# Series of products with a moving operand taken by turns, put behind the last product of a two-layer model

## The chip, the cores and the metric

The kernel runs on one core of one Trainium2 chip. The metric is the device time of one execution in microseconds. All of the work is in float32, and nearly all products use the fp32r form of it, in which one instruction streams a moving operand of up to 512 columns through a stationary operand of 128 × 128.

## The reference

The model has two layers over 256 tokens of width 1024, with a memory of another 256 tokens. Every layer has four parts, each followed by a layer normalisation:

```python
for l in range(DEPTH):
    h = layer_norm(ALPHA * h + 0.5 * swiglu(h, ffn1_gate[l], ffn1_up[l], ffn1_down[l]), ln_g[l, 0], ln_b[l, 0])
    z = h @ w_in[l]
    cb, cc, ch, rq, rf, ri, rg, pu = jnp.split(z, split_at, axis=-1)
    y_conv = short_gated_conv(ch, cb, cc, conv_w[l])
    y_rec = hgrn2(rq, rf, ri, rg, lbs[l], rec_norm_g[l])
    y_pool = multiscale_pool(pu, pool_w[l], pool_scale[l])
    mix = jnp.concatenate([y_conv, y_rec, y_pool], axis=-1) @ w_out[l]
    h = layer_norm(ALPHA * h + mix, ln_g[l, 1], ln_b[l, 1])
    h = layer_norm(ALPHA * h + cross_attn(h, mem, ca_q[l], ca_k[l], ca_v[l], ca_o[l]), ln_g[l, 2], ln_b[l, 2])
    h = layer_norm(ALPHA * h + 0.5 * swiglu(h, ffn2_gate[l], ffn2_up[l], ffn2_down[l]), ln_g[l, 3], ln_b[l, 3])
return h
```

`swiglu` is `(silu(x @ w_gate) * (x @ w_up)) @ w_down` with an inner width of 2816. `hgrn2` is a gated recurrence over the tokens, `multiscale_pool` takes running means over 2, 4, 8 and 16 tokens, and `cross_attn` attends to the memory with four heads.

## The kernel before

Every float32 operand is kept as two fp32r tiles, a high part and what is left of it, the low part (`split`, lines 59 and 60: ScalarE rounds the high part, VectorE subtracts it). A product of two such operands is made of three: high by high, high by low and low by high.

The activations `h` (two tiles of 128 tokens) are transposed by TensorE into `xT`, a tile of 128 partitions by 8 slices of 128 features, each with the high part of 256 tokens and then the low part of 256 tokens. `mT` holds the memory in the same way. So one slice of `xT` or `mT` is a run of 512 elements in a partition: elements 0 to 255 are the high part and 256 to 511 the low part.

```python
xT = cst.tile([P, NK, 2, SEQ], F32R, name="xT")
mT = cst.tile([P, NK, 2, SEQ], F32R, name="mT")
```

The weights come from memory by the queue of SP, in pieces of 1 MB, into three rotating tiles `raw`, and are split into `whi` and `wlo`. Two helpers make most products. `mm_cols` (lines 97 to 100) has the weights stationary and one slice of `xT` moving: eight products of 512 columns by the high weights (both parts of the activations at once) and eight of 256 columns by the low weights, into one PSUM tile, whose two halves are added afterwards. `mm_rows` (lines 109 to 111) has the activations stationary and 512 columns of the weights moving. In both, the moving operand is one unbroken run of elements in each partition, and so is the output in PSUM. Every product loads its stationary operand anew.

Inside the recurrence (line 578) TensorE also multiplies plain fp32 operands of 128 columns; there the moving operand is a view of `q` in runs of 1, 2, 4 and up to 64 elements, one length for each of seven levels, with gaps of the same length between the runs.

PSUM has four buffers with the tag `acc` and four with the tag `dn`, each of 512 float32 columns, which take turns. A planner orders the instructions of each engine by their dependencies; where `tc.manual_schedule` names an engine, its instructions stay in the order in which they are written.

The last thing that the kernel computes is `finish` (from line 247) of the second feed-forward part of layer 1. It makes the last products of the down projection for the first 128 tokens, normalises these and writes them out, and does the same for the other 128 tokens, where the last 512 columns are made in two pieces of 256 (lines 231 to 235). After the last of these products TensorE has no more work, while VectorE finishes the second normalisation and the output is written by the queues of SP and ScalarE (line 294).

Of the kernel before, what the change touches and what calls it, by code (L numbers as in the profile page):

```python
# [14 lines left out]
E = mybir.EngineType  # L15
PSUM = bass.MemoryType.PSUM

P = 128
# [783 lines left out]
        pend = ffn(l, "ffn2", 3, pend, last=l == DEPTH - 1)  # L802


# [1 line left out]
_INS = [  # L806
    "x", "mem", "ffn1_gate", "ffn1_up", "ffn1_down", "w_in", "conv_w", "rec_lb", "rec_norm_g", "pool_w",
# [22 lines left out]
```

## Time and profile before

| | |
|---|---|
| time, median of 2 runs | 1176.38 us (1175.93 to 1176.84) |
| time of the profiled execution | 1176.58 us |
| span of the profiled execution | 1174.8 us |
| mean granted clock of TensorE | 0.998 |
| TensorE products | 6219, busy 1161.9 us |
| TensorE weight loads | 6219, busy 1001.2 us |
| VectorE busy | 824.7 us |
| ScalarE busy | 595.6 us |
| moved by DMA | 218.23 MB |

Lines of a group have the line of the kernel, the engine, the operation, the output and the inputs by the program's names, the shapes and the number of instructions; behind these stand the busy time and the mean of one. Lines in order of time have the start in us from the span's start, the duration in us, the engine and then the same names. "acc<-xT,whi" is a product into a tile `acc` with `xT` moving and `whi` stationary. Records of products overlap, since one product starts before the last column of the one before it has reached PSUM: the time that a product costs in a stream is the distance between two starts.

### The profile page before, as it was taken

What the parts mean: (1) busy time and instruction counts of PE and PEld (TensorE: products, weight loads), DVE (VectorE), ACT (ScalarE), POOL (GpSimd) and SP (SyncE); (2) the same over time, 40 slices, a digit from 0 to 9 for tenths busy, and PEclk for the clock granted to TensorE, in tenths of its full rate; (3) what the DMA queues carried; (4) which work ended last, traced back from release to release, by engine and by line L of the source; (5) the groups of instructions that cost most, each with busy time, mean ns of one, the idle gap of its engine ahead of it and who ended that gap; (6) DMA issues with size and microseconds to landing.
All of it is one profiled execution on the core that took longest, in us unless ns stands there. A gap on an engine that the chain in (4) does not pass through costs nothing.

```text
span 1174.8 us, 15745 instructions
## 1 busy us (share of the span) xinstructions
PE 1161.9 (99%) x6219; PEld 1001.2 (85%) x6219; DVE 824.7 (70%) x1194; ACT 595.6 (51%) x873; POOL 40.1 (3%) x80
## 2 busy tenths in 40 slices
PE   8999999999999999999999999999999999999997
PEld 6888888888889888888888888888888888888886
DVE  5766567889787666566677665687998777665665
ACT  6555553626456355455355555446354653554550
POOL 7000000000000000000000000000000000000000
PEclk9999999999999999999999999999999999999999
DMA  8655564644474375655466544655255545655440
GB/s 327 252 193 201 174 221 143 220 140 151 172 244 167 96 247 180 215 198 196 144 215 221 202 168 169 228 187 194 73 209 183 212 144 177 217 179 203 164 171 36
DMA packets 98522, 218.23 MB, mean 186 GB/s; under 512 B 3792, under 2 KB 16368, under 8 KB 98448
## 3 DMA queue, kind: packets, MB, share of 16 engines
q1 hardware_dynamic: 97968, 216.68, 53.2%
q8 instruction: 49, 0.80, 0.3%
q10 hardware_dynamic: 288, 0.39, 0.1%
q14 instruction: 25, 0.20, 0.0%
q0 software_dynamic: 192, 0.15, 0.0%
HBM read 216.15 MB, written 1.05 MB: 185 GB/s over the span
## 4 chain that ended last, share of the span: by engine, by line
PE 97%; DVE 2%; DMA 0%; ACT 0%; issue 0%; SPq 0%; DVEq 0%; ACTq 0%
PE acc L97 29%; PE acc L99 17%; PE dn L111 10%; PE dn L109 10%; PE dn L110 9%; PE acc L109 5%; PE acc L110 5%; PE acc L111 5%; PE acc L100 4%; PE acc L149 1%; PE dn L578 1%; DMA raw<-in_ffn_gate_dram 0%; DVE wlo L60 0%; DVE AT L597 0%; PE dn L621 0%; PE acc L759 0%
## 5 line engine op out<-in xcount | busy, mean ns | idle before, releaser
L60 DVE TENSOR_TENSOR wlo<-raw,whi 128x1024 fp32r<-128x1024 f32 (+1 forms) x396 | 471.1, 1209 | 129.7 <-ACT whi L59 73.6
L59 ACT CAST whi<-raw 128x1024 fp32r<-128x1024 f32 (+1 forms) x396 | 399.7, 1043 | 208.2 <-PE dn L111 140.9
L97 PE MATMUL acc<-xT,whi 128*128 128x512 f32 x1400 | 358.5, 393 | 0.0
L97 PEld LDWEIGHTS acc<-xT,whi 128*128 128x128 f32 x1400 | 262.2, 188 | 50.3
L99 PEld LDWEIGHTS acc<-xT,wlo 128*128 128x128 f32 x1600 | 218.3, 190 | 15.5
L99 PE MATMUL acc<-xT,wlo 128*128 128x256 f32 x1600 | 223.5, 282 | 0.0
L109 PE MATMUL dn<-whi,ah 128*128 128x512 f32 x346 | 135.3, 391 | 0.0
L111 PE MATMUL dn<-whi,al 128*128 128x512 f32 x346 | 134.8, 389 | 0.0
L110 PE MATMUL dn<-wlo,ah 128*128 128x512 f32 x346 | 134.6, 389 | 0.0
L105 DVE TENSOR_TENSOR sg<-acc,sg 128x256 f32<-128x256 f32 x72 | 30.4, 422 | 78.4 <-ACT sg L104 78.4
L100 PE MATMUL acc<-xT,whi 128*128 128x512 f32 x200 | 79.2, 396 | 0.0
L111 PEld LDWEIGHTS dn<-whi,al 128*128 128x128 f32 x346 | 64.9, 188 | 13.7
L110 PEld LDWEIGHTS dn<-wlo,ah 128*128 128x128 f32 x346 | 65.0, 188 | 13.5
L109 PEld LDWEIGHTS dn<-whi,ah 128*128 128x128 f32 x346 | 65.1, 188 | 12.6
L104 ACT COPY sg<-acc 128x256 f32<-128x256 f32 x72 | 26.6, 370 | 94.7 <-PE acc L100 94.7
L109 PE MATMUL acc<-whi,xT 128*128 128x512 f32 x160 | 63.4, 397 | 0.1
L110 PE MATMUL acc<-wlo,xT 128*128 128x512 f32 x160 | 63.0, 393 | 0.0
L111 PE MATMUL acc<-whi,xT 128*128 128x512 f32 x160 | 62.8, 392 | 0.0
L104 ACT COPY up<-acc 128x256 f32<-128x256 f32 x72 | 26.6, 370 | 59.8 <-PE acc L100 59.8
L105 DVE TENSOR_TENSOR up<-acc,up 128x256 f32<-128x256 f32 x72 | 30.3, 421 | 31.8 <-ACT up L104 31.8
L109 PE MATMUL dn<-whi,xT 128*128 128x512 f32 x128 | 50.3, 393 | 0.0
L111 PE MATMUL dn<-whi,xT 128*128 128x512 f32 x128 | 49.9, 390 | 0.0
(202 smaller groups left out, 1236.9 us busy)
## 6 DMA issues: line engine op xcount, KB each, us to landing
raw<-in_ffn_up_dram SPq DMA_DIRECT2D x44, 1024.0 KB, 5.0
raw<-in_ffn_down_dram SPq DMA_DIRECT2D x44, 1024.0 KB, 4.8
raw<-in_ffn_gate_dram SPq DMA_DIRECT2D x42, 1024.0 KB, 5.0
raw<-in_w_in_dram SPq DMA_DIRECT2D x24, 1024.0 KB, 5.0
raw<-in_ca_k_dram SPq DMA_DIRECT2D x8, 1024.0 KB, 4.9
raw<-in_w_out_dram SPq DMA_DIRECT2D x8, 1024.0 KB, 4.8
raw<-in_ca_v_dram SPq DMA_DIRECT2D x8, 1024.0 KB, 5.6
raw<-in_ca_q_dram SPq DMA_DIRECT2D x8, 1024.0 KB, 4.9
```

The source lines that it names most:

```text
L59: nc.scalar.copy(hi, src)
L60: nc.vector.tensor_tensor(lo, src, hi.bitcast(F32), op=ALU.subtract)
L97: nc.tensor.matmul(o, w.at(k, cols)[0], x[:, k], start=k == 0, stop=False)
L99: nc.tensor.matmul(o[:, 0, :], w.at(k, cols)[1], x[:, k, 0, :], start=False, stop=False)
L100: nc.tensor.matmul(o, w.at(NK - 1, cols)[0], x[:, NK - 1], start=False, stop=True)
L104: nc.scalar.copy(dst, view(o[:, 1, :]))
L105: nc.vector.tensor_tensor(dst, view(o[:, 0, :]), dst, op=ALU.add)
L109: nc.tensor.matmul(o, xh, wh, start=start, stop=False)
L110: nc.tensor.matmul(o, xh, wl, start=False, stop=False)
L111: nc.tensor.matmul(o, xl, wh, start=False, stop=stop)
L149: nc.tensor.transpose(pt[:, k, :], src[:, (4 * j + k) * P : (4 * j + k + 1) * P], unit)
L578: nc.tensor.matmul(o[:, hh], kc[:, hh, :], view(qf, hh * P + c, (other - c, 2), (2 * c, a), (1, c)), start=True, stop=True,)
```

## The change

Behind the two layers, a block is added in which TensorE runs products that write one PSUM tile `o` of 512 columns; nothing reads that tile. The stationary operand is always 128 columns of `xT` and the moving operand a view of `mT`, both as the run of the kernel has left them. A view is a list of (step, count) pairs, the outermost first. `series` makes 12 products of one kind, over six slices of `mT` and seven of `xT`; there are 24 calls. `turns`, which is `[(1, 256), (256, 2)]`, takes one element of the high part, one of the low part, the next of the high part, and so on: 512 columns in ones from two stretches. `both` does this in runs of `c` elements, for `c` = 2, 4, 8 and 16; the second call for each `c` gives the output the same order, so that every column lands where it would have without the turns. Four further series take ones from stretches that are 16, 32, 64 and 128 elements apart. One takes pairs from two slices, 512 apart. Five have 256 columns, two of them in pairs (of which one is in effect an unbroken run) and three in ones. Three series have a stationary operand with a step of two elements: with `turns`, with an unbroken run, and with 256 columns in ones. The last series has 128 columns in one run.

After the series come 48 products: `h` stands for eight of 512 columns in `turns`, `n` for eight of 256 columns in ones with other stationary columns; first they alternate, and then they run in the order h, n, h, n by eights.

```diff
+    x1, m1 = (a.rearrange("p k h s -> p (k h s)") for a in (xT, mT))
+
+    def view(t, at, dims):
+        return bass.AP(tensor=t.tensor, offset=t.offset + at, ap=[list(t.ap[0])] + [list(d) for d in dims])
+
+    def series(dims, odims=None, n=12, w=((1, P),), slow=False):
+        ncol = 1
+        for d in dims:
+            ncol *= d[1]
+        for k in range(n):
+            b = 512 * (k % 6)
+            out = view(o, 0, odims or [(1, ncol)])
+            nc.tensor.matmul(out, view(x1, 512 * (k % 7), w), view(m1, b, dims), start=True, stop=True)
+
+    with tc.manual_schedule(engines={E.PE}):
+        o = acc((P, 512))
+        turns = [(1, 256), (256, 2)]
+        series([(1, 512)])
+        series(turns)
+        for c in (2, 4, 8, 16):
+            both = [(c, 256 // c), (256, 2), (1, c)]
+            series(both)
+            series(both, both)
+        series([(32, 16), (1, 16), (16, 2)])
+        series([(64, 8), (1, 32), (32, 2)])
+        series([(128, 4), (1, 64), (64, 2)])
+        series([(256, 2), (1, 128), (128, 2)])
+        series([(2, 128), (512, 2), (1, 2)])
+        series([(1, 128), (256, 2)])
+        series([(1, 128), (128, 2)])
+        series([(2, 128), (1, 2)])
+        series([(2, 64), (128, 2), (1, 2)])
+        series([(32, 8), (1, 16), (16, 2)])
+        series(turns, w=((2, 128),))
+        series([(1, 512)], w=((2, 128),))
+        series([(1, 128), (128, 2)], w=((2, 128),))
+        series([(1, 128)])
+        h = [(view(o, 0, [(1, 512)]), view(x1, 512 * (k % 7), [(1, P)]), view(m1, 512 * k, turns)) for k in range(8)]
+        n = [
+            (view(o, 0, [(1, 256)]), view(x1, 512 * (k % 7) + 256, [(1, P)]), view(m1, 512 * k, [(1, 128), (256, 2)]))
+            for k in range(8)
+        ]
+        for m in [m for k in range(8) for m in (h[k], n[k])] + h + n + h + n:
+            nc.tensor.matmul(*m, start=True, stop=True)
```

## The prediction

> **What bounds the kernel now.** I read the page from the top: the busy shares, the clock row of the 40 slices, and the chain that ended last.
>
> ```profile
> span 1174.8 us, 15745 instructions
> PE 1161.9 (99%) x6219; PEld 1001.2 (85%) x6219; DVE 824.7 (70%) x1194; ACT 595.6 (51%) x873; POOL 40.1 (3%) x80
> PEclk9999999999999999999999999999999999999999
> ...
> PE 97%; DVE 2%; DMA 0%; ACT 0%; issue 0%; SPq 0%; DVEq 0%; ACTq 0%
> ```
>
> TensorE is busy for 99% of the span and makes 97% of the chain. Whatever is put on its queue lengthens the kernel, unless it fits where TensorE is idle. So I asked for the waits of TensorE, and for the order of time around its last product.
>
> ```profile
> PE acc L149 <- DMA h<-in_x_dram: 4.8, 3, 3.4
> PE dn L578 <- DVE kc L572: 0.6, 2, 0.3
> ```
>
> Its waits are 5.4 us in all, most of them at the start. The only other idle stretch is behind the last product:
>
> ```profile
> 1163.01 0.28 PE L109 MATMUL acc<-whi,ah 128*128 128x256 f32 x1
> ...
> 1167.21 0.28 PE L111 MATMUL acc<-whi,al 128*128 128x256 f32 x1
> 1167.52 0.42 DVE L269 TENSOR_TENSOR h<-h,acc 128x256 f32<-128x256 f32 x1 [1.27 <-PE acc L111]
> 1167.98 0.43 DVE L279 BATCH_NORM_STATS2 st<-h 128x6 f32<-128x256 f32 x1
> ...
> 1170.13 1.54 DVE L291 SCALAR_TENSOR_TENSOR h<-h,rs,lnb 128x512 f32<-128x512 f32 x3
> 1170.90 1.13 SPq L294 DMA_DIRECT2D out_dram<-h  x2
> ```
>
> The last product starts at 1167.21 and its record ends at 1167.49; the last normalisation and the write of the output follow until 1174.8. These 7.3 us are the cover of the added work: the new products read nothing that the tail writes, and the tail reads nothing of theirs.
>
> **What is added.** Nothing is removed or moved. Each of the 24 series has 12 products. By the number of moving columns (the product of the counts in the pattern): 17 series have 512 columns, 6 have 256 and one has 128. The mixed run at the end has three rounds of the eight `h` (512 columns) and the eight `n` (256 columns). That makes 17 × 12 + 24 = **228 products of 512 columns**, 6 × 12 + 24 = **96 of 256** and **12 of 128**, together 336, each with its own weight load.
>
> The price of one is the distance from start to start, not the duration of a record, since records overlap. For 512 columns, from a stretch where the products follow each other without a wait:
>
> ```profile
> 1123.26 0.40 PE L109 MATMUL dn<-whi,ah 128*128 128x512 f32 x1
> ...
> 1133.93 0.39 PE L111 MATMUL dn<-whi,al 128*128 128x512 f32 x1
> ```
>
> These are the first and the last of 48 such rows: 10.67 us in 47 steps, 0.227 us each. For 256 columns the rows at 1163.01 and 1167.21 above are the first and the last of 36: 4.20 us in 35 steps, 0.120 us each. The difference is 0.107 us for 256 columns, or 0.418 ns a column, on top of some 0.013 us that each product costs. For 128 columns of this type there is no row. The nearest is the decay product, of plain fp32, which leaves two records for each product:
>
> ```profile
> 836.18 1.05 PE L578 MATMUL dn<-q,kc 128*128 128x128 f32 x8
> 836.99 0.48 PE L97 MATMUL acc<-xT,whi 128*128 128x512 f32 x1
> ```
>
> Eight records in 0.81 us are 0.101 us each. The formula of the longer ones gives 0.067, and the row at 0.101 has weight loads beside it as the new ones will; I take 0.101 (12 products: 1.2 us; by the formula 0.8).
>
> If every column comes at the rate of before, the sum is 228 × 0.227 + 96 × 0.120 + 1.2 = 51.8 + 11.5 + 1.2 = **64.5 us**.
>
> **What the order of the moving operand costs.** This is the open term. In before all products of fp32r read their moving operand in one piece, so no row shows the change's pattern. In ones, each element comes from another place than its neighbour: series 2 and 11 to 14 and the one with `turns` and stepped weights, 6 × 12 + 24 `h` = 96 products of 512 columns; and series 16, 17, 20 and 23 (the second-last), 4 × 12 + 24 `n` = 72 of 256 columns. If an element taken alone costs twice a column's time, that adds 96 × 0.214 + 72 × 0.107 = 20.5 + 7.7 = **28.2 us**; if four times, 84.7; if nothing, 0.
>
> Two rows stand near. The decay product reads its moving operand with a step of two elements in its first level and in runs of up to 64 later. Its first and its last level cost alike:
>
> ```profile
> 247.20 1.15 PE L578 MATMUL dn<-q,kc 128*128 128x128 f32 x8
> 264.32 1.05 PE L578 MATMUL dn<-q,kc 128*128 128x128 f32 x8
> ```
>
> That speaks for no cost, but not strongly: an fp32 record of 128 columns takes 0.101 us, 0.79 ns a column, about twice the 0.418 of fp32r, so a reading that delivers half the elements would be hidden there; and its elements are neighbours at two steps, not 16 to 256 apart. The other row is VectorE's masked copy, whose runs grow with the level; the rows are those of levels 1, 2, 4 and 16:
>
> ```profile
> 249.00 1.32 DVE L597 COPY_PREDICATED AT<-masks,dn 128x256 f32<-128x256 uint8 x2
> 251.35 1.32 DVE L597 COPY_PREDICATED AT<-masks,dn 128x256 f32<-128x256 uint8 x2
> 254.85 0.76 DVE L597 COPY_PREDICATED AT<-masks,dn 128x256 f32<-128x256 uint8 x2
> 260.01 0.76 DVE L597 COPY_PREDICATED AT<-masks,dn 128x256 f32<-128x256 uint8 x2
> ```
>
> Short runs cost 1.32 against 0.76, 1.7 times. So the two nearest rows say between once and about twice; half the rate is also the only slower rate at which a row shows TensorE taking columns. I take twice, and keep once and four times (half of a half) as ends.
>
> [...]
>
> **Pairs and longer runs.** Three series of 512 columns in pairs (`c` = 2 twice, and the one 512 apart) and one of 256: I take nothing. Bounds: nothing, and twice, 36 × 0.214 + 12 × 0.107 = 9.0 us. Runs of 4, 8 and 16: nothing, for the masked copy's rows already stand at 0.76 from four on. **Written by turns** (the four `series(both, both)`): no row of before has TensorE write PSUM in another order than one piece. Bounds: nothing and twice, 48 × 0.214 = 10.3 us; I take nothing, for the shortest written run is a pair. None of these can be a gain: 0.418 ns a column is the shortest in the trace. **Weights with a step of two** (36 loads): a load lasts 0.19 us and a product follows in 0.120 us with its load hidden, so a load twice as dear still ends within two products; I take nothing, at most 36 × 0.1 = 3.6 us.
>
> **Waits.** All 336 products write one PSUM buffer, in TensorE's own order, so they wait for nobody. Of the four buffers of its tag it gets the one that an `up` product of the last chunk used some 20 us earlier. Should it instead wait for the reader at L269 (ends 1167.94), that is 0.6 us. Nobody waits for the new products. Their instructions are 672 on a queue that already issues more than 12,000 at this rate.
>
> **The sum.** The first new product starts one step after the last old one, at 1167.21 + 0.12 = 1167.33. The stream takes 64.5 + 28.2 = 92.7 us, and the last record (256 columns in ones) reaches 0.16 us beyond its step: 1260.2. The tail ends at 1174.8 and no longer counts. Behind TensorE's end I count nothing; before had 3.1 us from the last VectorE instruction (1171.67) to the end, in which the output landed, so at most that. The profiled execution took 1176.58 us, 1.8 more than its span: 1260.2 + 1.8 = **1262.0 us**. It lies 0.2 above the median of 1176.38, so the forecast against the median is +85.4 us, 7.3%. A measurement of this kernel can tell about 2% (23.5 us) from no change.
>
> **The rivals.**
> *The order of reading is free* (L578's rows speak for it): 1167.3 + 64.5 + 0.2 + 1.8 = 1233.8 us. Chance 18%.
> *Ones cost twice, and pairs or written turns too*: up to 9.0 + 10.3 more, 1271 to 1281 us. [...] Chance 17%.
> *Ones cost three to four times*, if a place gives its elements at a quarter of the rate: 56.4 to 84.7 us in place of 28.2, 1290 to 1319, with pairs at twice 1328. No row shows TensorE so slow. Chance 23%.
> *The new products run closer together than the old*, since none adds to the one before it: at the pace of a 256-column product for all, 324 × 0.120 + 1.2 = 40.1 us, 1209 us. The decay products don't add up either, and come no closer than 0.101. [...] Chance 2%.
> *Not slower, because most of the products aren't executed*: nobody reads their results, and a builder that drops such work would leave before's time, 1176.6. Within 2% the stream may end at 1174.8 + 23.5 = 1198.3, 31.0 us after its start; at 64.5 / 336 = 0.192 us each, that is 161 products. From fewer than 161 executed it isn't slower. Against it: the program's output isn't what places work on TensorE's queue in a kernel written instruction by instruction. Chance 2%.
>
> The forecast itself keeps 38%. The range takes in the free order at its low end and, above, the costs of pairs and writes and ones at three times with a part of them: **1232 to 1300 us**, which leaves out four times, closer products and the dropped work, some 2 in 10. Faster by over 2%: 1%; within 2%: 2%; slower: 97%.
>
> **What would show it.** In the changed profile TensorE should have 6555 products and a tail in which it alone works. Step from start to start: 0.227 in the first series; 0.44 in the second if ones cost twice; 0.227 for `c` = 2 and up, read or written; 0.44 for the distances 16 to 128; 0.227 for 256 columns in ones; at most 0.101 for 128 columns. The clock should stay at full through the tail; a drop would make all of it dearer and the prediction wrong, and so would a cost that depends on the distance of the stretches.

## The result and the profile after

The changed kernel takes 1238.31 us (median of 2 runs, 1236.89 to 1239.73) where the kernel before takes 1176.38: a ratio of 1.0526 (95% interval 1.0472 to 1.0581), 62 us more. The forecast was 1262 within 1232 to 1300, so the sign and the range held, and the size came out near the low end of the range. The profiled execution took 1239.73 us, 1.7 more than its span.

The page of the changed kernel, its busy shares and the chain that ended last:

```profile
span 1238.0 us, 16417 instructions
PE 1231.8 (99%) x6555; PEld 1058.2 (85%) x6555; DVE 825.1 (67%) x1194; ACT 595.5 (48%) x873; POOL 40.1 (3%) x80
...
PEclk9999999999999999999999999999999999999999
...
PE 97%; DVE 2%; DMA 0%; ACT 0%; SPq 0%; issue 0%; ACTq 0%
```

TensorE has the 336 products more and nearly 70 us more of busy time; VectorE (825.1 beside 824.7 us) and ScalarE (595.5 beside 595.6) are as they were, and the granted clock stays at full (a mean of 1.000). In order of time, TensorE alone (start, duration, line, count):

```profile
1167.81 0.28 PE L111 MATMUL acc<-whi,al 128*128 128x256 f32 x1
1167.93 61.19 PE L817 MATMUL acc<-mT,xT 128*128 128x512 f32 x288
1228.95 8.07 PE L848 MATMUL acc<-mT,xT 128*128 128x512 f32 x48
```

The new products begin 0.12 us after the last old one, without a wait, and run until 1228.95 + 8.07 = 1237.02: 69.1 us. The forecast's sum was 92.7, and 64.5 without any cost of the order of reading. The groups by line, with the forms kept apart (busy time, mean ns of one record), show which of the products differ:

```profile
L817 PE MATMUL acc<-mT,xT 128*128 128x512 f32 x204 | 51.2, 414 | 0.0
...
L848 PE MATMUL acc<-mT,xT 128*128 128x512 f32 x24 | 6.5, 382 | 0.0
```

The mean record of 512 columns lasts 414 ns in the series and 382 in the mixed run, whose products of 512 columns are all in ones, and 389 to 397 in the kernel before. A record's length isn't the price, but it speaks against dear ones: their records are shorter than those of products in one piece. Something else in the series is longer.

### The profile page after: what moved, and what is told of

Same layout as the page of the kernel before. It is cut to its first block, busy times and chain, and to the rows that moved or that the text cites. A ratio compares the mean times of both kernels' runs of the same rounds, so it can differ in the third digit from the quotient of the medians.

```text
span 1238.0 us, 16417 instructions
## 1 busy us (share of the span) xinstructions
PE 1231.8 (99%) x6555; PEld 1058.2 (85%) x6555; DVE 825.1 (67%) x1194; ACT 595.5 (48%) x873; POOL 40.1 (3%) x80
## 4 chain that ended last, share of the span: by engine, by line
PE 97%; DVE 2%; DMA 0%; ACT 0%; SPq 0%; issue 0%; ACTq 0%
PE acc L97 27%; PE acc L99 16%; PE dn L111 9%; PE dn L109 9%; PE dn L110 9%; PE acc L817 5%; PE acc L109 5%; PE acc L110 5%; PE acc L111 5%; PE acc L100 4%; PE acc L149 1%; PE dn L578 1%; PE acc L848 1%; DMA raw<-in_ffn_gate_dram 0%; DVE wlo L60 0%; DVE AT L597 0%
## 5 line engine op out<-in xcount | busy, mean ns | idle before, releaser
L99 PE MATMUL acc<-xT,wlo 128*128 128x256 f32 x1600 | 223.5, 282 | 0.0
L817 PE MATMUL acc<-mT,xT 128*128 128x512 f32 (+2 forms) x288 | 61.2, 377 | 0.0
L817 PEld LDWEIGHTS acc<-mT,xT 128*128 128x128 f32 x288 | 49.3, 192 | 11.8
```

The source lines that it names most:

```text
L99: nc.tensor.matmul(o[:, 0, :], w.at(k, cols)[1], x[:, k, 0, :], start=False, stop=False)
L817: nc.tensor.matmul(out, view(x1, 512 * (k % 7), w), view(m1, b, dims), start=True, stop=True)
```

## The experiments

Each added series of experiments 1, 2, 3 and 5 stands behind the last product of the kernel before, in the way of the change, but on a line of its own, so that the order of time gives a start for each. A product's cost is the difference of two starts divided by the 12 products. The line numbers behind `#` are those of the run's kernel; `...` stands for lines left out.

**Experiment 1: which patterns cost.**

```diff
+        for a in series(turns): mm(*a, start=True, stop=True)                                # L829
+        for a in series(runs(2)): mm(*a, start=True, stop=True)                              # L830
+        for a in series(runs(2), runs(2)): mm(*a, start=True, stop=True)                     # L831
+        for a in series(runs(4)): mm(*a, start=True, stop=True)                              # L832
...
+        for a in series([(4, 128), (1, 2), (2, 2)]): mm(*a, start=True, stop=True)           # L841
+        for a in series([(8, 64), (1, 4), (4, 2)]): mm(*a, start=True, stop=True)            # L842
...
+        for a in series([(2, 512)]): mm(*a, start=True, stop=True)                           # L844
+        for a in series([(4, 512)], every=5): mm(*a, start=True, stop=True)                  # L845
+        for a in series([(8, 256)], every=5): mm(*a, start=True, stop=True)                  # L846
...
+        for a in series([(1, 256), (0, 2)]): mm(*a, start=True, stop=True)                   # L848
+        for a in series([(1, 128), (128, 4)]): mm(*a, start=True, stop=True)                 # L849
+        for a in series([(4, 256), (1, 2)]): mm(*a, start=True, stop=True)                   # L850
+        for a in series([(8, 128), (1, 4)]): mm(*a, start=True, stop=True)                   # L851
...
+        for a in series(runs(4), at=1): mm(*a, start=True, stop=True)                        # L854
```

> The kernel before with 34 series of 12 products behind its last product, each series on a line of its own, so that each has a start in the order of time. The first thirteen repeat the change's: 0.216 us a product for every series in ones, 0.227 in one piece, 0.340 for pairs, 0.250, 0.243 and 0.240 for runs of 4, 8 and 16. New are ones that are 2, 4 and 8 elements apart, steps of 2, 4 and 8 without turns, a descending operand, each element twice, ones from four stretches, runs with gaps in one stretch, starts moved by 1 or 2 elements, and runs of 32, 64 and 128. Theory 'neighbours' (a column costs more when it lies at the address behind the column before it): every pattern without neighbours costs 0.216, at any distance, with steps of 2, 4 and 8 too; runs of 2, 4 and 8 with gaps cost the same as by turns (0.340, 0.250, 0.243). Theory 'change of stretch' (the cost comes where a run ends and the other stretch goes on): runs with gaps in one stretch cost 0.227, runs of 32, 64 and 128 fall towards 0.227 (0.234, 0.230, 0.228). [...]

TensorE in order of time:

```profile
1169.16 2.75 PE L829 MATMUL acc<-mT,xT 128*128 128x512 f32 x12
1171.74 4.24 PE L830 MATMUL acc<-mT,xT 128*128 128x512 f32 x12
1175.81 4.25 PE L831 MATMUL acc<-mT,xT 128*128 128x512 f32 x12
1179.89 3.18 PE L832 MATMUL acc<-mT,xT 128*128 128x512 f32 x12
1182.90 3.17 PE L833 MATMUL acc<-mT,xT 128*128 128x512 f32 x12
...
1206.68 2.90 PE L841 MATMUL acc<-mT,xT 128*128 128x512 f32 x12
1209.42 2.75 PE L842 MATMUL acc<-mT,xT 128*128 128x512 f32 x12
1212.01 2.75 PE L843 MATMUL acc<-mT,xT 128*128 128x512 f32 x12
1214.60 5.66 PE L844 MATMUL acc<-mT,xT 128*128 128x512 f32 x12
1220.08 5.71 PE L845 MATMUL acc<-mT,xT 128*128 128x512 f32 x12
1225.61 2.79 PE L846 MATMUL acc<-mT,xT 128*128 128x256 f32 x12
1228.23 2.99 PE L847 MATMUL acc<-mT,xT 128*128 128x512 f32 x12
1231.05 2.75 PE L848 MATMUL acc<-mT,xT 128*128 128x512 f32 x12
1233.64 3.55 PE L849 MATMUL acc<-mT,xT 128*128 128x512 f32 x12
1237.03 5.58 PE L850 MATMUL acc<-mT,xT 128*128 128x512 f32 x12
1242.43 2.98 PE L851 MATMUL acc<-mT,xT 128*128 128x512 f32 x12
1245.24 2.96 PE L852 MATMUL acc<-mT,xT 128*128 128x512 f32 x12
```

Ones by turns (L829) take 2.58 / 12 = 0.215 us, pairs (L830) 0.339, pairs that are also written by turns (L831) 0.340, runs of four (L832) 0.251. One step inside a single stretch is far dearer than any turns: a step of 2 (L844) 0.457, a step of 4 (L845) 0.461, a step of 8 with 256 columns (L846) 0.218, so the same per column. As they stand, both theories fall. "Neighbours" wanted 0.216 for steps of 2, 4 and 8; they cost double. "Change of stretch" wanted 0.227 for pairs with gaps in one stretch (L850); they cost 0.450.

What puts the rows in order is a count. Lay the elements of a slice out in fours (0 to 3, 4 to 7 and so on), take the columns of even number alone, and count how many elements in a row come from the same four; in these rows the columns of odd number give the same count:

| pattern | the even columns take | in a row | us for 512 columns |
|---|---|---|---|
| ones 256 or 4 apart, each twice (L829, L842, L848) | 0, 1, 2, 3 | 4 | 0.216 |
| one piece; ones 2 apart (L841) | 0, 2, 4, 6 and 0, 1, 4, 5 | 2 | 0.227, 0.228 |
| runs of four with gaps (L851) | 0, 2, 8, 10 | 2 | 0.234 |
| step of 2; pairs with gaps (L844, L850) | 0, 4, 8 | 1 | 0.457, 0.450 |
| step of 4 (L845) | 0, 8, 16 | 1 | 0.461 |
| four stretches in ones (L849) | a0, c0, a1, c1 | 1, four visits by turns | 0.283 |
| pairs by turns (L830) | a0, b0, a2, b2 | 1, two visits by turns | 0.339 |

Other sizes than four don't order the rows: in twos, one piece and a step of 2 would count alike, at 0.227 and 0.457, and in eights a step of 2 and runs of four with gaps, at 0.457 and 0.234. It also fits that runs of four that begin one or two elements late, and so lie across two fours, cost 3.99 / 12 = 0.333 (L854, from 1252.03 to 1256.02; L855, to 1260.02) where runs of four that begin on a four cost 0.251. It doesn't account for all of the latter: in runs of four and longer, by turns, the even columns take at least two in a row, which gives 0.227, and runs of 4, 8, 16 and 32 cost 0.251, 0.243, 0.240 and 0.236 (L832, L834, L836, L858). From 64 on they cost 0.228 and 0.227 (L859, L860), about as "change of stretch" had it for long runs. So a change of stretch seems to cost something of its own; how is open.

The count is fitted to these times; no record shows how the operand is fetched.

**Experiment 2: is it the weight load that meets the reading?**

```diff
+        for a in series(one, w=[(1, 128)]): mm(*a, start=True, stop=True)                    # L828
+        for a in series(turns, w=[(1, 128)]): mm(*a, start=True, stop=True)                  # L829
...
+        for a in series(one, w=[(1, 32)], rows=32): mm(*a, start=True, stop=True)            # L840
+        for a in series(turns, w=[(1, 32)], rows=32): mm(*a, start=True, stop=True)          # L841
+        for a in series(runs(2), w=[(1, 32)], rows=32): mm(*a, start=True, stop=True)        # L842
```

> The kernel before with 18 series behind its last product: a stationary operand of 128, 64 and 32 columns, each with a moving operand in one piece, by turns in ones, in pairs and in runs of four (512 columns) and in one piece and in ones of 256 columns. Theory 'meeting' (the extra time is where the reading of the moving operand and the load of the next weights meet, so it goes with the number of weights): with 64 and 32 columns one piece falls from 0.227 to 0.221 and 0.218, pairs from 0.340 to 0.278 and 0.247, runs of four from 0.250 to 0.233 and 0.224, and 256 columns in one piece from 0.120 to 0.115 and 0.112; ones stay at 0.216. Theory 'moving alone' (the extra belongs to the moving operand): all stay as with 128 columns, 0.227, 0.340 and 0.250.

```profile
1168.02 2.91 PE L828 MATMUL acc<-mT,xT 128*128 128x512 f32 x12
1170.76 2.75 PE L829 MATMUL acc<-mT,xT 128*128 128x512 f32 x12
...
1198.21 2.95 PE L840 MATMUL acc<-mT,xT 128*32 128x512 f32 x12
1201.00 2.75 PE L841 MATMUL acc<-mT,xT 128*32 128x512 f32 x12
1203.59 4.21 PE L842 MATMUL acc<-mT,xT 128*32 128x512 f32 x12
1207.62 3.13 PE L843 MATMUL acc<-mT,xT 128*32 128x512 f32 x12
```

With 32 in place of 128 weight columns one piece takes 0.233 (0.228 with 128), ones 0.216, pairs 0.336 (0.339 in experiment 1), where "meeting" wanted 0.218 for one piece and 0.247 for pairs. Of the rows that it wanted to shrink only 256 columns in one piece did so by its amount, from 0.119 to 0.115 with 64 weight columns (L832, L838), and with 32 they stayed there. So the extra of 512 columns, of pairs above all, belongs to the moving operand.

**Experiment 3: weights with a step, and short products.**

```diff
+        for a in series(one, w=[(2, 128)]): mm(*a, start=True, stop=True)                    # L830
...
+        for a in series([(1, 128)]): mm(*a, start=True, stop=True)                           # L842
...
+        for a in series([(1, 128)], w=[(2, 128)]): mm(*a, start=True, stop=True)             # L844
+        for a in series([(1, 128)], w=[(4, 128)]): mm(*a, start=True, stop=True)             # L845
+        for a in series([(1, 64)]): mm(*a, start=True, stop=True)                            # L846
...
+        for k, a in enumerate(series(one)): mm(*a, start=k == 0, stop=k == 11)               # L849
```

> The kernel before with 24 series behind its last product: a stationary operand with a step of 1, 2 and 4 elements beside a moving operand in one piece, in ones (two halves of each 256, 128 apart) and in pairs; the same with 256, 128 and 64 columns; and twelve products that add to one another, in one piece and in ones. Theory 'meeting': the step of the weights changes the extra of one piece and of pairs (0.233 with a step of two for one piece, more with four), and not that of ones (0.216). Theory 'moving alone': one piece 0.227 and pairs 0.340 at every step. With 128 and 64 columns the weight load sets the pace: 0.112 at both widths with a step of one, and if a step makes the load itself slower, more than that. Adding up changes nothing: 0.227 and 0.216.

```profile
1201.64 1.45 PE L842 MATMUL acc<-mT,xT 128*128 128x128 f32 x12
1202.93 1.50 PE L843 MATMUL acc<-mT,xT 128*128 128x128 f32 x12
1204.26 1.58 PE L844 MATMUL acc<-mT,xT 128*128 128x128 f32 x12
1205.68 2.96 PE L845 MATMUL acc<-mT,xT 128*128 128x128 f32 x12
1208.48 1.52 PE L846 MATMUL acc<-mT,xT 128*128 128x64 f32 x12
```

A product of 128 columns takes 1.29 / 12 = 0.108 to 0.111 (L842, L843), and one of 64 columns as much (L846 to the next start at 1209.81: 0.111): the number of moving columns makes no difference there, but the step of the weights does. With a step of 2 a product takes 0.118 (L844), with a step of 4 0.233 (L845), so the load of 128 weights sets the pace. At steps of 1, 2 and 4 its elements, counted over all columns, come four, two and one in a row from the same four, and the times stand in the order of experiment 1's count. Beside 512 columns in one piece the step costs little (0.233 with a step of 2, 0.236 with 4; L830, L833). "Moving alone" wanted 0.227 at every step, so this small part went as "meeting" had it. With a step of 4 the load itself, at 0.233, sets the pace, for ones too (0.237, L834). With a step of 2 the load, at 0.118, is short enough, and ones stay at 0.216 (L831); why one piece takes some 0.005 more is open.

The twelve products that add up in one piece (L849) took 5.09 us, 0.424 each, where 0.227 was expected. The granted clock of that stretch is 0.52; experiment 5 has the same series at 0.228 (L845), just ahead of a stretch with a clock of 1.00 (1195 to 1200). The stretches are those of the series; the columns are the length, the busy time and count, the clock, and the DMA:

```profile
1204.26:1208.40 4.14, 4.14 (x26) 1.00 0.00 0
1208.50:1212.30 3.80, 3.80 (x25) 0.67 0.02 4
1212.40:1215.10 2.70, 2.70 (x13) 0.50 0.00 0
1215.15:1220.20 5.05, 5.05 (x13) 0.52 0.00 0
```

**Experiment 4: the change without its pairs.**

```diff
-            both = [(c, 256 // c), (256, 2), (1, c)]
+            both = [(c, 256 // c), (256, 2), (1, c)] if c > 2 else [(1, 512)]
...
-            series(both, both)
+            series(both, both if c > 2 else None)
...
-        series([(2, 128), (512, 2), (1, 2)])
+        series([(1, 512)])
...
-        series([(2, 64), (128, 2), (1, 2)])
+        series([(1, 256)])
```

> The change with its four series in pairs (three of 512 columns, one of 256) read and written in one piece; all the rest as it is. If pairs cost what the trace of the changed kernel shows, 36 products go from 0.337 to 0.227 and 12 from 0.166 to 0.120: 4.5 us less, 1233.8 us. If instead the pairs' time belonged to their place in the order (other engines still at work on the tail while they run), the products in one piece there would be as slow, and the time would stay at 1238.

Measured: 1234.24 us (1232.51 to 1235.27), 1.0491 of the kernel before (1.0473 to 1.0508); the span went from 1238.0 to 1233.5. That is 4.1 us less by the medians and 4.5 by the spans. The intervals of the two ratios overlap, so the ratios alone don't separate the kernels. The rows do:

```profile
1167.97 56.69 PE L817 MATMUL acc<-mT,xT 128*128 128x512 f32 x288
1224.50 8.07 PE L848 MATMUL acc<-mT,xT 128*128 128x512 f32 x48
```

The series take 1224.50 − 1167.97 = 56.53 us, and in the changed kernel 1228.95 − 1167.93 = 61.02: 4.5 us, as forecast. The pairs' time was theirs, and not that of their place in the order.

**Experiment 5: the count, in patterns not yet seen.**

```diff
+        for a in series([(2, 256), (512, 2)], every=5): mm(*a, start=True, stop=True)        # L840
+        for a in series([(4, 256), (1024, 2)], every=4): mm(*a, start=True, stop=True)       # L841
+        for a in series([(3, 256), (1024, 2)], every=4): mm(*a, start=True, stop=True)       # L842
+        for a in series([(1, 128), (256, 4)], every=5): mm(*a, start=True, stop=True)        # L843
+        for a in series([(2, 128), (256, 4)], every=5): mm(*a, start=True, stop=True)        # L844
+        for k, a in enumerate(series(one)): mm(*a, start=k == 0, stop=k == 11)               # L845
+        for k, a in enumerate(series(turns)): mm(*a, start=k == 0, stop=k == 11)             # L846
+        for a in half([(1, 512)]): mm(*a, start=True, stop=True)                             # L847: xT, mT as bf16
+        for a in half([(1, 256), (512, 2)]): mm(*a, start=True, stop=True)                   # L848
+        for a in half([(2, 512)]): mm(*a, start=True, stop=True)                             # L849
+        for a in half([(4, 512)]): mm(*a, start=True, stop=True)                             # L850
+        for a in half([(2, 128), (512, 2), (1, 2)]): mm(*a, start=True, stop=True)           # L851
```

> The kernel before with 18 series behind its last product. [...] Two series add their twelve products up, in one piece and in ones: 0.227 and 0.216 if the 0.427 that such a series in one piece took elsewhere was the clock, which stood at 0.52 there, and 0.427 again if adding up is what costs.

```profile
1172.64 2.91 PE L840 MATMUL acc<-mT,xT 128*128 128x512 f32 x12
1175.39 5.59 PE L841 MATMUL acc<-mT,xT 128*128 128x512 f32 x12
1180.81 4.34 PE L842 MATMUL acc<-mT,xT 128*128 128x512 f32 x12
1184.98 3.45 PE L843 MATMUL acc<-mT,xT 128*128 128x512 f32 x12
1188.27 4.16 PE L844 MATMUL acc<-mT,xT 128*128 128x512 f32 x12
1192.26 2.90 PE L845 MATMUL acc<-mT,xT 128*128 128x512 f32 x12
1195.00 2.75 PE L846 MATMUL acc<-mT,xT 128*128 128x512 f32 x12
1197.59 2.77 PE L847 MATMUL acc<-mT,xT 128*128 128x512 bf16 x12
1200.19 5.97 PE L848 MATMUL acc<-mT,xT 128*128 128x512 bf16 x12
1206.00 2.87 PE L849 MATMUL acc<-mT,xT 128*128 128x512 bf16 x12
1208.71 5.58 PE L850 MATMUL acc<-mT,xT 128*128 128x512 bf16 x12
1214.12 3.43 PE L851 MATMUL acc<-mT,xT 128*128 128x512 bf16 x12
1217.39 6.64 PE L852 MATMUL acc<-mT,xT 128*128 128x512 bf16 x12
```

For fp32r the count holds in all five, with the price of the row in experiment 1 that it puts beside each: turns with a step of 2 (two in a row) take 0.229 (0.227 there), with a step of 4 (one) 0.452 (0.457), with 3 (one or two) 0.348 (between these), four stretches (one, four visits by turns) 0.274 (0.283), the same with a step of 2 (one, two visits by turns) 0.333 (0.339). The form of turns from two stretches doesn't set the price by itself: with steps of 1, 2, 3 and 4 it took 0.216, 0.229, 0.348 and 0.452. Adding up costs nothing here: 0.228 in one piece, beside 0.229 for the same products alone (L838, from 1167.30 to 1170.05), and 0.216 in ones.

For bf16, with elements of half the bytes, the author's estimate was the same count in eights. That agrees with one piece (0.217), with steps of 2 (0.226) and 4 (0.451) and with pairs by turns (0.273, beside the 0.283 of four visits), but not with ones by turns, 0.484 in place of 0.216 (L848), nor with the turns with a step of 2 (0.54 in place of 0.216, L852; the next series starts at 1223.87). Three stretches took 0.51 (L853); four took 0.80 (L854), most of it at a granted clock of 0.50. So the count doesn't carry over to elements of two bytes; why is open, and was followed no further, since this kernel's products are of four bytes.

**Experiment 6: the kernel before, reading by turns.** Ones are cheaper than one piece (0.216 against 0.227 us), so the kernel's own products were given that order. The products write PSUM in one piece in the order in which columns come; ScalarE and VectorE take every second column when they read.

```diff
+    def tw(a):
+        return a.rearrange("p (a s) -> p s a", a=2)
+    def place(o):
+        return o.rearrange("p (s a) -> p s a", a=2)
+    def un(o):
+        return o.rearrange("p (s a) -> p a s", a=2)
...
-            nc.tensor.matmul(o, w.at(k, cols)[0], x[:, k], start=k == 0, stop=False)
+            nc.tensor.matmul(full, w.at(k, cols)[0], both_parts(k), start=k == 0, stop=False)
...
-            nc.tensor.matmul(o[:, 0, :], w.at(k, cols)[1], x[:, k, 0, :], start=False, stop=False)
+            nc.tensor.matmul(place(o[:, 0, :]), w.at(k, cols)[1], tw(x[:, k, 0, :]), start=False, stop=False)
...
-        nc.scalar.copy(dst, view(o[:, 1, :]))
-        nc.vector.tensor_tensor(dst, view(o[:, 0, :]), dst, op=ALU.add)
+        nc.scalar.copy(dst, un(o[:, 1, :]))
+        nc.vector.tensor_tensor(dst, un(o[:, 0, :]), dst, op=ALU.add)
```

`full` and `both_parts(k)` are `o` and `x[:, k]` with tokens 0 to 127 and 128 to 255 by turns within each part.

> The kernel before, without any added product, in which the products with the weights stationary read the activations by turns from tokens 0 to 127 and 128 to 255, in ones; the sums lie in PSUM in that order, and the instructions that read them take every second column. By the series, 1728 products of 512 columns go from 0.227 to 0.216 and 1728 of 256 columns from 0.120 to 0.112: 19 + 14 = 33 us less, 1143 us, ratio 0.972. Rival: ScalarE and VectorE read PSUM with a step of two more slowly and become the bound in these stages, then less gain or a loss. Rival: products that come from freshly split weights and add up don't follow the series; then 1176.

Measured: 1143.62 us (1142.34 to 1144.29), ratio 0.9725 (0.9711 to 0.9738): 32.4 us less than the kernel before beside it (1175.98), where 33 were expected. Both rivals are out: a copy of 128 × 256 out of PSUM by ScalarE takes 371 ns (370 before), VectorE's addition 422 as before, and products that add up follow the series. Then the products with the activations stationary as well:

```diff
-        nc.tensor.matmul(o, xh, wh, start=start, stop=False)
+        nc.tensor.matmul(place(o), xh, tw(wh), start=start, stop=False)
...
-                        h[i][:, c], h[i][:, c], ALPHA / scale, y[i][n], op0=ALU.mult, op1=ALU.add
+                        by2(h[i][:, c]), by2(h[i][:, c]), ALPHA / scale, un(y[i][n]), op0=ALU.mult, op1=ALU.add
```

> As before, and the products with the activations stationary read the weights by turns from both halves of their columns as well: another 2094 products of 512 columns from 0.227 to 0.216 and 228 of 256 columns from 0.120 to 0.112, 23 + 2 = 25 us. Together 58 us less than before, 1118 us, ratio 0.951. Rival: the outputs that are read with a step of two make the layer normalisation's reads slower, which stand on the path at the end of each part; a doubled read of 0.68 us in 14 places would give back some 10 us.

Measured: **1120.26 us** (1119.42 to 1121.86), ratio 0.9529 (0.9516 to 0.9542), 55.7 us less. In its code `by2` views a row as its two halves, to match the order in which `un` reads. By groups, the first with line 97 of before, the second with line 99, and the read of the sums by VectorE with line 275 (by-form groups and groups of this kernel):

```profile
L114 PE MATMUL acc<-xT,whi 128*128 128x512 f32 x1400 | 339.9, 381 | 0.9 <-DVE xT L60 0.6 <-DVE sg L123 0.3
L116 PE MATMUL acc<-xT,wlo 128*128 128x256 f32 x1600 | 211.3, 275 | 0.0
...
L293 DVE SCALAR_TENSOR_TENSOR h<-h,dn 128x512 f32<-128x512 f32 x31 | 21.2, 683 | 32.1 <-PE dn L129 32.1
```

The 1400 went from 358.5 to 339.9 us of busy time and the 1600 from 223.5 to 211.3. The read with a step of two still takes 683 ns, as before (x31, 21.2 us): that rival is out. The chain shows what begins to follow:

```profile
PE 87%; DVE 8%; DMA 2%; issue 1%; ACT 1%; SPq 0%; DVEq 0%; ACTq 0%
```

TensorE's share of it fell from 97% to 87%. Of the 2 us that miss from the 58, waits of TensorE such as those in L114's row are a likely part: they sum to 5.4 us before and 7.0 here.

## Why the prediction was right, and where it was wrong

**The bound and the place: right.** TensorE's queue decides the end; the new products start 0.12 us after the last one, wait for nobody, and nobody waits for them.

**The count and the base: right.** 336 products; one piece at 0.227 and 256 columns at 0.120, as read off before. 128 columns take 0.108 to 0.111, said 0.101, and the limit is the weight load (0.233 with its step of 4), as the choice of the row supposed. But "some 0.013 us that each product costs" was read as a fixed price of an instruction. With 512 columns 0.011 of it belongs to reading in one piece: in ones a product takes 0.216.

**The order of reading: wrong, and this is the step that failed.** "I take twice" for elements taken alone put 28.2 us on the sum. Measured is a gain: 96 products × (0.216 − 0.227) = −1.1 us, and 72 × (0.112 − 0.120) = −0.6. The factor came from VectorE's masked copy (1.7 times) and from the half rate of plain fp32, and neither held for TensorE reading fp32r. What makes ones cheaper no run shows; by the count they take four elements in a row from the same four where one piece takes two. The sentence "None of these can be a gain: 0.418 ns a column is the shortest in the trace" looked at the columns alone; the gain came out of the rest. The caution about L578 was right: in fp32r a step of two does cost double (0.457). That the plain fp32 rows hid it wasn't tested; the weight load, which holds 128 columns of fp32r at 0.108 to 0.111, may do so. Those rows were also compared by their durations: by starts the first level took 0.90 us (247.20 to 248.10) and the last 0.81 (264.32 to 265.13), so they aren't quite alike.

**Pairs: taken at nothing, wrong.** No run shows pairs by turns at nothing: they cost 0.340 (0.333 with the two slices 512 apart, L840), within the bounds given (nothing to twice): 24 × 0.113 + 12 × 0.106 + 12 × 0.046 = 4.5 us, as experiment 4 has it. **Runs of 4, 8 and 16: taken at nothing**, and they cost 0.250, 0.243 and 0.240, together 24 × (0.023 + 0.016 + 0.013) = 1.2 us; VectorE's masked copy didn't hold here either. **Written by turns: right**, nothing (L830 beside L831). **Stepped weights: right** within the bound, 0.006 for one piece, 0.007 for 256 columns in ones (experiment 3, L837 and L840) and nothing for 512 in ones: together 0.2 us.

**The sum put right:** 64.5 − 1.7 + 4.5 + 1.2 + 0.2 = 68.7 beside 69.1 us measured; the last record's 0.16 us beyond its step is in the latter. The start was 0.6 us later than supposed, as the whole kernel ahead of it was, and the program's end took 1.0 us behind TensorE (1237.02 to 1238.0), which was counted at nothing.

**The rivals.** "The order of reading is free" (18%, 1233.8) is nearest to the time, but not what happened: the order has gains of 1.7 us and losses of 5.7. The range held because its low end had been set by this rival; the forecast's own term of 28.2 us isn't in the time, so that it held isn't owed to the mechanism. Ones at two, three or four times are out, and so are dear written turns, in runs of two and more (pairs written by turns 0.340, beside 0.339 in one piece; runs of four 0.250, beside 0.251). "Closer together" is out (no series of 512 columns took less than 0.215), and so is "not executed" (6555 products). Of the signs that were named, 0.44 for ones would have shown the forecast right; the rows show 0.216; the clock stayed at full (1.000), and the distance of the stretches made no difference from 4 to 256.

## What to carry to other kernels

Price a product by the distance between starts, and don't take the part that doesn't grow with the columns for a fixed fee: a change in how the operand is read can take it away. For fp32r the rows here follow a count, made for the even and the odd columns apart, of how many elements in a row come from the same four: four was best (0.216), two nearly as good (0.227 to 0.251), one cost double (0.450 to 0.461), or about one and a half times (0.333 to 0.340) where pairs came by turns; four stretches in ones, also one, took 0.274 to 0.283. The count is fitted to the times of fp32r, not a shown mechanism, and it fails for bf16. In this kernel all stretches of 512 columns could be read as two halves by turns, and the readers of PSUM could take every second column: TensorE's busy time got 5% shorter (1161.9 to 1102.8 us), and the kernel, which TensorE bounds, took 4.7% less time. In bf16 the same order cost 0.484 in place of 0.217.

## What the runs showed that was not expected

- One piece isn't TensorE's fastest order for fp32r: 0.227 us for 512 columns against 0.216 in ones by turns; in bf16 one piece takes 0.217.
- The granted clock fell to 0.50 in experiment 3 while the records show TensorE busy without a gap. It fell in the series of 64 columns (0.67 from 1208.50 to 1212.30, 0.50 behind it). The series of 512 columns behind them still ran at 0.52, each product taking 0.424 us, and the next at full (1.00) again. In experiment 5 it fell to 0.50 as well, in the four bf16 stretches (L854, 0.80 us a product), with 0.52 for the series of 512 columns behind them; in experiment 1, with products of 0.457 us, the mean over the run was 1.0. What lowered it no run shows.
- A step of 4 elements in the stationary operand doubles its load (0.233 against 0.108 to 0.111 us); beside 512 moving columns in one piece that is nearly hidden (0.236).
